# Fourier mixing by five products instead of six, border sums without a product of zeros, and one selection for layer 1's scale and shift

## The chip, the core and the metric

The kernel runs on one core of a Trainium2 chip. The metric is the time of one execution on the device in microseconds, the median of several runs. TensorE (PE) multiplies, VectorE (DVE) and ScalarE (ACT) work elementwise, GpSimd (POOL) does little here, SyncE (SP) issues most of the DMAs.

## The reference

Two layers of a diffusion trunk over 256 latent and 256 context tokens of width 2048. Each layer normalises, applies a scale and a shift that come from the conditioning vectors, projects, and mixes in three branches whose gated outputs go through one output projection:

```python
shift, scale, gate = jnp.split(silu_c @ w_mod[l] + b_mod[l], 3, axis=-1)
h = rmsnorm(x, g_pre[l]) * (1.0 + scale[:, None]) + shift[:, None]
proj = h @ w_in[l]                      # split into branches A, B, C and their gates
...
def fourier_mix(xc, w_f, b_f):          # branch C
    xg = xc.reshape(bsz, t, C_GROUPS, C_DIM).astype(jnp.float32)
    y = jnp.fft.fft2(xg, axes=(1, 3), norm='ortho').real.astype(xc.dtype)
    y = jnp.einsum('btgc,gcd->btgd', y, w_f) + b_f
...
y = rmsnorm(y @ w_out[l], g_post[l]);  x = x + gate[:, None] * y
```

The context stream gets the same in layer 0; in layer 1 it gives only keys and values.

## The kernel before

All activations lie transposed (features on partitions, 512 columns: latent, then context). Precision comes from splits: `split_into` writes the float32r high part of a float32 tensor with ScalarE (line 562 in the profile) and the low part by a subtraction on VectorE (line 563), and `mm3` multiplies high by high, high by low and low by high (lines 545, 546, 547). Weights arrive by DMA as `raw`, are split into `whi` (L513) and `wlo` (L515), and `tunit` or, in layer 1, `tunit1` (L692, L693) multiplies one unit of 128 output columns by all 16 tiles of the input.

TensorE works in program order. What isn't the main stream of units is put in between by `Later`: generators such as `fourier`, `attention`, `mod_end` and `boundary` yield a number, the time in microseconds of the main stream after which their next piece is issued. `YF` holds `fourier`'s numbers (3.4 us between the first and second stage in layer 0, 6.4 us in layer 1). On VectorE, ScalarE and SP the order after the first stage is made by priorities; every engine's queue is then in order.

Branch C's 2-D transform is two stages. `fourier_mats` multiplies the cosine and the sine matrix by the group's weight matrix, once per layer, and keeps high and low parts in `mg` and `mgl`. `fourier(g, ps)` runs once per group (4) and layer. It adds and subtracts mirrored positions (L1015), so that an even half `e` and an odd half `o` of 128 positions each stand for 256 positions, and splits them. Then for each stream (two in layer 0, one in layer 1) the first stage multiplies each half by cosine and sine together, 256 columns, by `mm3`: six products into the tile `ps_f`. Of the four blocks of 128 columns that come out, the second stage uses even by cosine, odd by sine, and of odd by cosine a single row, which takes the place of row 0 of the odd-by-sine block. A split of the two blocks and a split of the one row follow (ACT and DVE, each one operation of 128x256 and one of 1x128), and `ps_z` is six more products: three by `ct`, three by `nst`, the last of which needs the row's subtraction.

Layer 1's shift and scale and layer 0's gate are vector work: `mod_dve` multiplies 512 columns of `w_mod` with VectorE, at a low priority (`macc`, L292 and L294, with transposes and reductions into `red`, L300 and L301), as DMAs bring `mraw`. Four such blocks fill a `red` tile. `mod_end` then selects and turns them by eight small products (four `PE.matmul` of float32, two instructions each; tile `ps_modc`, L314), and `mod_cols` adds biases (L151, L155, L157). It is issued `MODEND` microseconds of main stream after the last block: 53 in layer 0, 45 in layer 1. It runs three times: for layer 0's gate, layer 1's scale (`gs`) and layer 1's shift (`sh`). The first layer-1 product needs both, in `make_h` (L623, L632).

Sums over features come from products with a column of ones: `col_sums` (L581, L583), called in `rms_of` for the context stream between the layers (twice), and the same by hand in `boundary` (L1359, L1362). Both open the accumulation with a product of ones by zeros over all columns, and add each column's product to it.

Of the kernel before, what the change touches and what calls it, by code (L numbers as in the profile page):

```python
# [7 lines left out]
F32 = mybir.dt.float32  # L8
F32R = mybir.dt.float32r
BF16 = mybir.dt.bfloat16  # L10
AF = mybir.ActivationFunctionType
ALU = mybir.AluOpType

P = 128
# [52 lines left out]
def trunk_kernel(ctx: ExitStack, tc: tile.TileContext, xT, xhalf, cT, wss, wsl, wmod, win, wout0, wout1, const, vec, rows,  # L67
                 wmat, bs, sink, out):
    nc = tc.nc
    V, A, G, PE, DMA = nc.vector, nc.scalar, nc.gpsimd, nc.tensor, nc.sync  # L70
# [6 lines left out]
    def sb(shape, dt, tag, bufs=1):  # L77
        cnt[0] += 1
        return pool.tile(shape, dt, tag=tag, bufs=bufs, name=f"{tag}_{cnt[0]}")
# [8 lines left out]
    def ms_ps(name="ms"):  # L88
        cnt[0] += 1
        return psum.tile([P, 512], F32, tag="ms", bufs=2, name=f"ps_{name}_{cnt[0]}")  # L90
# [6 lines left out]
    ones = sb([P, P], F32, "ones")  # L97
# [4 lines left out]
    zero8 = sb([P, 8], F32, "zero8")  # L102
    V.memset(zero8, 0.0)
    zero4 = zero8[:, 0:4]
# [22 lines left out]
    def cc(name):  # L127
        o, w = COFF[name]
        return cst[:, o - P:o - P + w]
# [151 lines left out]
    def mod_dve(l, cb, red):  # L281

        acc = sb([P, 2, 512], F32, "macc")
        for kg in range(4):
            for kk in range(4):
                if kk % 2 == 0:
                    w = sb([P, 2, 512], F32, "mraw", 2)
                    DMA.dma_start(w, wmod[(cb - 8) if l == 0 else 4 + cb, kg][:, kk:kk + 2])
                for s in range(2):
                    c = cs[:, kg * 4 + kk, s:s + 1]  # L290
                    if kg == 0 and kk == 0:
                        V.tensor_scalar(out=acc[:, s], in0=w[:, kk % 2], scalar1=c, scalar2=None, op0=ALU.mult)  # L292
                    else:
                        V.scalar_tensor_tensor(out=acc[:, s], in0=w[:, kk % 2], scalar=c, in1=acc[:, s],  # L294
                                               op0=ALU.mult, op1=ALU.add)
                if kk % 2 and (kg < 3 or kk < 3):
                    yield
        t = sb([P, 2, 512], F32, "mraw", 2)
        for s in range(2):
            V.transpose(t[:, s], acc[:, s])  # L300
            V.tensor_reduce(out=red[:, s], in_=t[:, s].rearrange("p (b j) -> p b j", j=32),  # L301
                            axis=mybir.AxisListType.X, op=ALU.add)
        yield

    def mod_four(l, cbs):
        red = sb([P, 4, 2, 16], F32, "red", 2)
        for i, cb in enumerate(cbs):
            yield from mod_dve(l, cb, red[:, i])
        later.add(mod_end(l, cbs, red), MODEND[l])

    def mod_end(l, cbs, red):
        ps = ms_ps("modc")
        for q in range(4):
            PE.matmul(ps[32 * q:32 * q + 32, 0:32], cc("selq"),  # L314
                      red.rearrange("p c s (j q) -> p c s j q", q=4)[:, :, :, :, q], start=True, stop=True,
                      tile_position=(0, 32 * q))
        for i, cb in enumerate(cbs):
            mod_cols(l, cb, ps[:, 8 * i:8 * i + 8].rearrange("p (s j) -> p j s", s=2))
        yield 0.0

# [30 lines left out]
        yield 0.0  # L351

    def mod_rest():
        yield from mod_four(0, range(8, 12))
        yield from mod_four(1, range(4, 8))
        yield from mod_four(1, range(0, 4))
        while "acc" not in state:
            yield
        yield from mod_gate1()
# [23 lines left out]
    MODEND = 53.0, 45.0  # L383
# [41 lines left out]
    later = Later()  # L425
# [118 lines left out]
    def mm3(ps, st, mv, start, stop):  # L544
        PE.matmul(ps, st[0], mv[0], start=start, stop=False)  # L545
        PE.matmul(ps, st[0], mv[1], start=False, stop=False)  # L546
        PE.matmul(ps, st[1], mv[0], start=False, stop=stop)  # L547

    def part(w, c):

        def of(t):
            if not isinstance(t, list):
                return t[:, c]
            n = t[0].shape[-1]
            return t[c.start // n][:, c.start % n:c.start % n + c.stop - c.start]

        return of(w[0]), of(w[1])
# [3 lines left out]
    def split_into(hi, lo, src):  # L561
        A.copy(hi, src)  # L562
        V.tensor_tensor(out=lo, in0=src, in1=hi.bitcast(F32), op=ALU.subtract)  # L563
        return hi, lo
# [10 lines left out]
        G.tensor_tensor(out=r[:, :n], in0=t[:, :n], in1=mhalf[:, :n], op=ALU.pow)  # L575
        return r

    def col_sums(ps, q, n, start=True, stop=True):

        if start:  # L580
            PE.matmul(ps[:, 0:n], ones, zero4[:, 0:n], start=True, stop=False)  # L581
        for j in range(n):
            PE.matmul(ps[:, j:j + 1], q[:, j * P:(j + 1) * P], ones[:, 0:1], start=False, stop=stop and j == n - 1)  # L583

    wz = sb([P, T], BF16, "join", 2)

# [137 lines left out]
    def layer(l):  # L724
        last = l == 1
        n = S if last else T
# [3 lines left out]
        if last:  # L730
            a = sb([P, 4, 256], F32, "macc")
            c = [sb([P, 2, S], F32, f"kt{j}") for j in range(2)]
# [50 lines left out]
        if l == 0:  # L783
            mod = {}
            for k in range(KT):
# [42 lines left out]
                m = mod.get(k + 1)  # L828
# [160 lines left out]
                yield (4.0 if h == 1 else 2.0) if l == 0 else (7.0 if h == 1 else 2.0)  # L989


        mg = sb([P, 4, 2, P], F32R, "mg"), sb([P, 4, 2, P], F32R, "mgl")

        wfp = sb([P, 1024], F32R, "vv")
        wfp = split_into(wfp[:, 0:512], wfp[:, 512:1024], wf.rearrange("p g d -> p (g d)"))
# [3 lines left out]
        def fourier_mats():  # L999
            for j in range(2):  # L1000
                ps = ms_ps("mg")
                mm3(ps, csp[j], wfp, True, True)
                split_into(mg[0][:, :, j], mg[1][:, :, j], ps.rearrange("p (g d) -> p g d", d=P))
            yield 0.0

        def fourier(g, ps):


            e = w2k([P, n // S, 2, P])
            p2 = ps[:, 0:n].rearrange("p (s t) -> p s t", t=S)  # L1010
            A.copy(e[:, :, :, 0:1], ps[:, 0:n].rearrange("p (s j t) -> p s j t", j=2, t=P)[:, :, :, 0:1])
            back = w2k([P, n // S, P])
            A.copy(back, p2[:, :, P:S])
            for j, op in enumerate((ALU.add, ALU.subtract)):
                V.tensor_tensor(out=e[:, :, j, 1:P], in0=p2[:, :, 1:P], in1=back[:, :, P - 1:0:-1], op=op)  # L1015
            x = split_into(w2k([P, n], F32R), w2k([P, n], F32R), e.rearrange("p s j t -> p (s j t)"))
            yield YF[l][0]
            z = mm_ps("z")
            mgg = [m[:, g].rearrange("p a b -> p (a b)") for m in mg]
            for s in range(n // S):  # L1020
                a = ms_ps("f1")
                for j in range(2):
                    t = 2 * s + j
                    mm3(a[:, j * 256:(j + 1) * 256], part(x, slice(t * P, (t + 1) * P)), mgg, True, True)
                a1 = w2k([P, 2, P], F32R), w2k([P, 2, P], F32R)
                split_into(*a1, a.rearrange("p (q d) -> p q d", d=P)[:, 0::3])
                split_into(a1[0][0:1, 1], a1[1][0:1, 1], a[0:1, 256:384])
                yield YF[l][1]
                zs = z[:, s * S:(s + 1) * S]
                for j, nm in enumerate(("ct", "nst")):  # L1030
                    mm3(zs, [m[:, j] for m in a1], split[nm], j == 0, j == 1)
            A.activation(ytmp(12 + g), z[:, 0:n], AF.Identity, bias=vc(l, "bf")[:, g:g + 1])
# [322 lines left out]
    def boundary(acc, cross):  # L1355


        ps = ms_ps("rs")
        PE.matmul(ps[:, 0:6], ones, zero8[:, 0:6], start=True, stop=False)  # L1359
        for i in range(6):  # L1360
            q = acc[:, i * P:(i + 1) * P] if i < 2 else cross[:, (i - 2) * P:(i - 1) * P]
            PE.matmul(ps[:, i:i + 1], q, ones[:, 0:1], start=False, stop=i == 5)  # L1362
        r = rstd_cols(ps[:, 0:2], 2, D)
        m, u = sb([P, 4], F32, "mx", 2), sb([P, 4], F32, "nm", 2)
        V.tensor_scalar(out=m[:, 0:2], in0=ps[:, 2:4], scalar1=2.0 / D, scalar2=None, op0=ALU.mult)
        V.tensor_scalar(out=m[:, 2:4], in0=ps[:, 4:6], scalar1=1.0 / D, scalar2=None, op0=ALU.mult)  # L1366
        for i, (x, op) in enumerate(((r[:, 0:2], ALU.mult), (m[:, 0:2], ALU.add), (r[:, 0:2], ALU.mult), (msx, ALU.add))):
            V.tensor_tensor(out=u[:, 0:2], in0=u[:, 0:2] if i else m[:, 2:4], in1=x, op=op)
        V.tensor_scalar(out=u[:, 0:2], in0=u[:, 0:2], scalar1=EPS, scalar2=None, op0=ALU.max)
        r1 = sb([P, 4], F32, "rs_b", 2)  # L1370
        G.tensor_tensor(out=r1[:, 0:2], in0=u[:, 0:2], in1=mhalf[:, 0:2], op=ALU.pow)
        yield YX[1]
        rb = bcast(r, 2)
        state["r0"] = sb([P, S], F32, "rbs", 2)
        A.copy(state["r0"], rb[:, 0:S])
        for k in range(NX):
            x1_of(k)
        yield YX[2]
        rb = bcast(r1, 2)
        rbs[0] = sb([P, S], F32, "rbs", 2)  # L1380
        A.copy(rbs[0], rb[:, 0:S])
# [54 lines left out]
    with tc.manual_schedule(engines={EN.PE}):  # L1436
# [11 lines left out]
        for k in range(KT):  # L1448
            q = w2k([P, T])
# [128 lines left out]
```

## Time and profile before

| | |
|---|---|
| median of 3 runs | 1126.23 us (1125.98 to 1126.52) |
| the profiled execution | 1126.57 us |
| its span in the trace | 1124.8 us |
| TensorE busy | 1116.0 us, 99% |
| VectorE busy | 919.9 us, 82% |
| ScalarE busy | 548.8 us, 49% |
| granted TensorE clock | 0.999 |

The profile is of one execution. A row of grouped instructions gives line, engine, operation, output and inputs, shapes and count; a row of the order of time gives start, duration, engine, line and operation, and in brackets how long the engine stood idle before it and for whom. `PEld` is TensorE's weight load. Matmul durations are pipelined: what one costs is the step to the next start, not its duration.

### The profile page before, as it was taken

The page shows a single profiled execution, that of the slowest core. Times are in us where ns is not written, and L with a number is a line of the kernel's source. Part 1 is how long each engine was busy: PE and PEld are TensorE (multiplying, and loading weights), DVE is VectorE, ACT ScalarE, POOL GpSimd, SP SyncE. Part 2 cuts the span into 40 slices and gives each one's busy share as a digit, 9 for nine tenths or more (in the row PEclk, how much of TensorE's full clock was granted, in tenths as well). Part 3 has the DMA queues.
Part 4 walks back from the last instruction along what each step waited for, and adds up shares of the span by engine and source line. Part 5 has one row for each costly group of instructions (what it writes and reads, how often), then busy time and mean ns, then how long its engine had stood idle before and what let it go on. Part 6 is the DMA issues. An engine that isn't in the chain of part 4 may idle for free.

```text
span 1124.8 us, 16564 instructions
## 1 busy us (share of the span) xinstructions
PE 1116.0 (99%) x6069; PEld 919.4 (82%) x6072; DVE 919.9 (82%) x1573; ACT 548.8 (49%) x1044; POOL 34.9 (3%) x44
## 2 busy tenths in 40 slices
PE   8999999999999999999999999999999999999998
PEld 3666788888888888888888888988888888898886
DVE  2667699899988897988998989396989689878883
ACT  5454723322335667632533334266665369867551
POOL 0000000000000000000000000030500000000000
PEclk9999999999999999999999999999999999999999
DMA  9999755576655343465566665285946686456872
GB/s 360 402 401 399 258 165 173 168 241 206 212 189 182 112 152 121 128 202 186 169 194 206 218 207 186 95 197 193 236 154 204 211 294 198 159 180 200 302 254 75
DMA packets 76002, 235.84 MB, mean 210 GB/s; under 512 B 8704, under 2 KB 13200, under 8 KB 75920
## 3 DMA queue, kind: packets, MB, share of 16 engines
q1 hardware_dynamic: 71136, 229.79, 60.7%
q0 software_dynamic: 4064, 3.69, 2.2%
q10 hardware_dynamic: 720, 1.31, 0.3%
q8 instruction: 47, 0.77, 0.3%
q14 instruction: 35, 0.29, 0.1%
HBM read 232.65 MB, written 2.10 MB: 209 GB/s over the span
## 4 chain that ended last, share of the span: by engine, by line
PE 88%; DVE 5%; DMA 3%; ACT 2%; issue 1%; ACTq 0%; POOLq 0%; DVEq 0%; SPq 0%
PE ps_t L545 14%; PE ps_t L547 14%; PE ps_t L546 14%; PE ps_t L692 9%; PE ps_t L693 5%; PE ps_av L771 4%; PE ps_v L1174 3%; PE ps_y L545 3%; PE ps_y L547 3%; PE ps_y L546 3%; PE ps_mod L182 2%; DVE macc L294 2%; DVE wlo L515 1%; PE ps_v L1175 1%; PE ps_tp L1116 1%; DMA mraw<-in_wmod_dram 1%
## 5 line engine op out<-in xcount | busy, mean ns | idle before, releaser
L513 ACT CAST whi<-raw 128x1024 fp32r<-128x1024 f32 (+1 forms) x209 | 215.9, 1037 | 314.7 <-PE ps_t L546 214.0
L545 PE MATMUL ps_t<-hh,whi 128*128 128x512 f32 (+1 forms) x752 | 290.7, 387 | 0.0
L515 DVE TENSOR_TENSOR wlo<-raw,whi 128x1024 fp32r<-128x1024 f32 (+1 forms) x209 | 250.4, 1202 | 48.3 <-ACT whi L513 40.5
L546 PE MATMUL ps_t<-hl,whi 128*128 128x512 f32 (+1 forms) x752 | 289.6, 385 | 0.0
L547 PE MATMUL ps_t<-hh,wlo 128*128 128x512 f32 (+1 forms) x752 | 289.4, 385 | 0.0
L294 DVE SCALAR_TENSOR_TENSOR macc<-mraw,cs,macc 128x512 f32<-128x512 f32 x360 | 250.5, 744 | 14.6 <-DMA mraw<-in_wmod_dram 14.1
L692 PE MATMUL ps_t<-hh,whi 128*128 128x512 f32 x512 | 184.6, 399 | 0.0
L547 PEld LDWEIGHTS ps_t<-hh,wlo 128*128 128x128 f32 x752 | 141.3, 188 | 28.7
L545 PEld LDWEIGHTS ps_t<-hh,whi 128*128 128x128 f32 x752 | 141.3, 188 | 26.7
L546 PEld LDWEIGHTS ps_t<-hl,whi 128*128 128x128 f32 x752 | 141.3, 188 | 26.3
L693 PE MATMUL ps_t<-hh,wlo 128*128 128x256 f32 x512 | 143.4, 280 | 0.0
L692 PEld LDWEIGHTS ps_t<-hh,whi 128*128 128x128 f32 x512 | 96.1, 188 | 21.2
L693 PEld LDWEIGHTS ps_t<-hh,wlo 128*128 128x128 f32 x512 | 96.7, 189 | 0.4
L545 PE MATMUL ps_y<-whi,hh 128*128 128x512 f32 x104 | 41.3, 397 | 0.0
L547 PE MATMUL ps_y<-whi,hh 128*128 128x512 f32 x104 | 40.6, 391 | 0.0
L546 PE MATMUL ps_y<-wlo,hh 128*128 128x512 f32 x104 | 40.5, 389 | 0.0
L562 ACT CAST w2k<-ps_tp 128x512 fp32r<-128x512 f32 x40 | 23.4, 584 | 21.2 <-PE ps_scc L546 13.7
L575 POOL TENSOR_TENSOR rs_b<-rs_a,mhalf 128x2 f32<-128x2 f32 (+1 forms) x6 | 6.7, 1115 | 759.5 <-DVE mx L1366 584.6
L563 DVE TENSOR_TENSOR w2k<-ps_tp,w2k 128x512 fp32r<-128x512 f32 x40 | 27.4, 684 | 3.5 <-ACT w2k L562 2.3
L1096 ACT ACTIVATE w2k<-w2k,den 128x512 f32<-128x512 f32 (+1 forms) x48 | 28.1, 647 | 0.7 <-DVE den L1091 0.6
L188 DVE STREAM_TRANSPOSE w2k<-ps_mod 128x256 f32<-128x256 f32 (+1 forms) x15 | 7.0, 468 | 26.1 <-PE ps_mod L182 24.5
L771 PE MATMUL ps_av<-whi,hh 128*128 128x512 f32 x64 | 24.6, 397 | 0.0
(483 smaller groups left out, 1819.3 us busy)
## 6 DMA issues: line engine op xcount, KB each, us to landing
raw<-in_win_dram SPq DMA_DIRECT2D x158, 512.0 KB, 4.1
mraw<-in_wmod_dram SPq DMA_DIRECT2D x128, 512.0 KB, 4.4
raw<-in_wout_dram SPq DMA_DIRECT2D x60, 512.0 KB, 4.5
mraw<-in_wsl_dram SPq DMA_DIRECT2D x12, 512.0 KB, 7.3
mg<-in_wsl_dram SPq DMA_DIRECT2D x7, 512.0 KB, 9.0
mgl<-in_wsl_dram SPq DMA_DIRECT2D x7, 512.0 KB, 9.0
yo<-in_xhalf_dram POOLq DMA_DIRECT2D x28, 128.0 KB, 7.2
yo<-in_xT_dram SPq DMA_DIRECT2D x12, 256.0 KB, 4.9
```

The lines of the kernel that those rows point to most:

```text
L294: V.scalar_tensor_tensor(out=acc[:, s], in0=w[:, kk % 2], scalar=c, in1=acc[:, s], op0=ALU.mult, op1=ALU.add)
L513: A.copy(ph, rc)
L515: self.last = V.tensor_tensor(out=pl, in0=rc, in1=ph.bitcast(F32), op=ALU.subtract)
L545: PE.matmul(ps, st[0], mv[0], start=start, stop=False)
L546: PE.matmul(ps, st[0], mv[1], start=False, stop=False)
L547: PE.matmul(ps, st[1], mv[0], start=False, stop=stop)
L563: V.tensor_tensor(out=lo, in0=src, in1=hi.bitcast(F32), op=ALU.subtract)
L692: PE.matmul(ps, w[0], h, start=k == 0, stop=False)
L693: PE.matmul(ps[:, 0:S], w[1], h[:, 0:S], start=False, stop=k == KT - 1)
L771: PE.matmul(ps, st[a], mv[b], start=start and (a, b) == (0, 0), stop=stop and (a, b) == (1, 0))
L1096: A.activation(prob[i][:, b * w:(b + 1) * w], prob[i][:, b * w:(b + 1) * w], AF.Copy, scale=den[:, c:c + 1])
L1174: PE.matmul(vps[t], hi, wk, start=k == 0, stop=False)
```

## The change

1. `fourier`'s first stage takes five products. The matrices are stored per pair of groups in the order sine high, cosine high, cosine low, sine low. The even half's high part is multiplied by cosine high and cosine low side by side (256 columns, blocks 0 and 1), its low part by cosine high alone (128 columns, added to block 0); even by sine is not formed. The odd half has its three products of 256 columns, into blocks 2 and 3. Block 1 is added to the low part of block 0's split by one VectorE operation. `fourier_mats` writes each product in two copies and two subtractions, one for each pair of groups.
2. `col_sums` and `boundary` lose the product of zeros; each column's product opens and closes its own accumulation.
3. Layer 1's scale and shift blocks are selected in one `mod_end`, at the place of the later one; layer 0's gate as before.

```diff
-    def mod_four(l, cbs):
-        red = sb([P, 4, 2, 16], F32, "red", 2)
-        for i, cb in enumerate(cbs):
-            yield from mod_dve(l, cb, red[:, i])
-        later.add(mod_end(l, cbs, red), MODEND[l])
-
-    def mod_end(l, cbs, red):
+    def mod_fours(l, *fours):
+        reds = []
+        for cbs in fours:
+            reds.append(sb([P, 4, 2, 16], F32, "red", 2))
+            for i, cb in enumerate(cbs):
+                yield from mod_dve(l, cb, reds[-1][:, i])
+        later.add(mod_end(l, fours, reds), MODEND[l])
+
+    def mod_end(l, fours, reds):
         ps = ms_ps("modc")
-        for q in range(4):
-            PE.matmul(ps[32 * q:32 * q + 32, 0:32], cc("selq"),
-                      red.rearrange("p c s (j q) -> p c s j q", q=4)[:, :, :, :, q], start=True, stop=True,
-                      tile_position=(0, 32 * q))
-        for i, cb in enumerate(cbs):
+        for i, red in enumerate(reds):
+            for q in range(4):
+                PE.matmul(ps[32 * q:32 * q + 32, 32 * i:32 * i + 32], cc("selq"),
+                          red.rearrange("p c s (j q) -> p c s j q", q=4)[:, :, :, :, q], start=True, stop=True,
+                          tile_position=(0, 32 * q))
+        for i, cb in enumerate(cb for cbs in fours for cb in cbs):
             mod_cols(l, cb, ps[:, 8 * i:8 * i + 8].rearrange("p (s j) -> p j s", s=2))
...
     def mod_rest():
-        yield from mod_four(0, range(8, 12))
-        yield from mod_four(1, range(4, 8))
-        yield from mod_four(1, range(0, 4))
+        yield from mod_fours(0, range(8, 12))
+        yield from mod_fours(1, range(4, 8), range(0, 4))
...
-    def col_sums(ps, q, n, start=True, stop=True):
-
-        if start:
-            PE.matmul(ps[:, 0:n], ones, zero4[:, 0:n], start=True, stop=False)
+    def col_sums(ps, q, n):
+
         for j in range(n):
-            PE.matmul(ps[:, j:j + 1], q[:, j * P:(j + 1) * P], ones[:, 0:1], start=False, stop=stop and j == n - 1)
+            PE.matmul(ps[:, j:j + 1], q[:, j * P:(j + 1) * P], ones[:, 0:1], start=True, stop=True)
...
-        mg = sb([P, 4, 2, P], F32R, "mg"), sb([P, 4, 2, P], F32R, "mgl")
+        mg = [sb([P, 2, 4, P], F32R, tag) for tag in ("mg", "mgl")]
...
                 mm3(ps, csp[j], wfp, True, True)
-                split_into(mg[0][:, :, j], mg[1][:, :, j], ps.rearrange("p (g d) -> p g d", d=P))
+                for i in range(2):
+                    split_into(mg[i][:, :, 1 - j], mg[i][:, :, 2 + j],
+                               ps[:, i * 256:(i + 1) * 256].rearrange("p (g d) -> p g d", d=P))
...
-            mgg = [m[:, g].rearrange("p a b -> p (a b)") for m in mg]
+            m = mg[g // 2][:, g % 2]
             for s in range(n // S):
-                a = ms_ps("f1")
-                for j in range(2):
-                    t = 2 * s + j
-                    mm3(a[:, j * 256:(j + 1) * 256], part(x, slice(t * P, (t + 1) * P)), mgg, True, True)
+                a = ms_ps("f1").rearrange("p (q d) -> p q d", d=P)
+                xe, xo = (part(x, slice(t * P, (t + 1) * P)) for t in (2 * s, 2 * s + 1))
+                PE.matmul(a[:, 0:2], xe[0], m[:, 1:3], start=True, stop=False)
+                PE.matmul(a[:, 0], xe[1], m[:, 1], start=False, stop=True)
+                mm3(a[:, 2:4], xo, (m[:, 0:2], m[:, 3:1:-1]), True, True)
                 a1 = w2k([P, 2, P], F32R), w2k([P, 2, P], F32R)
-                split_into(*a1, a.rearrange("p (q d) -> p q d", d=P)[:, 0::3])
-                split_into(a1[0][0:1, 1], a1[1][0:1, 1], a[0:1, 256:384])
+                split_into(*a1, a[:, 0::2])
+                V.tensor_tensor(out=a1[1][:, 0], in0=a1[1][:, 0].bitcast(F32), in1=a[:, 1], op=ALU.add)
+                split_into(a1[0][0:1, 1], a1[1][0:1, 1], a[0:1, 3])
...
         ps = ms_ps("rs")
-        PE.matmul(ps[:, 0:6], ones, zero8[:, 0:6], start=True, stop=False)
         for i in range(6):
             q = acc[:, i * P:(i + 1) * P] if i < 2 else cross[:, (i - 2) * P:(i - 1) * P]
-            PE.matmul(ps[:, i:i + 1], q, ones[:, 0:1], start=False, stop=i == 5)
+            PE.matmul(ps[:, i:i + 1], q, ones[:, 0:1], start=True, stop=True)
```

## The prediction

> **What bounds the kernel now.** I read the page's busy shares, the waits of TensorE, then the order of time around each edited place.
>
> ```profile
> span 1124.8 us, 16564 instructions
> PE 1116.0 (99%) x6069; PEld 919.4 (82%) x6072; DVE 919.9 (82%) x1573; ACT 548.8 (49%) x1044; POOL 34.9 (3%) x44
> PEclk9999999999999999999999999999999999999999
> PE ps_idle L590 <- DVE red L112: 2.0, 1, 2.0
> PE ps_x L1315 <- ACT w2k L1307: 0.5, 1, 0.5
> PE ps_z L547 <- DVE w2k L563: 0.2, 1, 0.2
> ```
>
> PE is busy in 99% of the span at a full granted clock throughout. The last three rows are three of PE's seven waits (engine, line, awaited instruction: total us, times, longest). The first and the four not shown, of 0.5 us and less, belong to the opening stage, L1315 to the last output tile. Between the two only one product waited, 0.2 us: the last of Fourier's second stage. So what a change takes out of PE's stream comes off the end, unless a product then waits for VectorE. All three parts are priced on PE; the extra work on VectorE is priced by whether a product waits for it.
>
> **Part 1, Fourier's products.** `fourier` multiplies per group and stream (8 times in layer 0, 4 in layer 1) six products of 256 moving columns now.
>
> ```profile
> 167.10 0.28 PE L545 MATMUL ps_f<-mg,w2k 128*128 128x256 f32 x1
> 167.69 0.28 PE L547 MATMUL ps_f<-mg,w2k 128*128 128x256 f32 x1
> 167.81 0.40 PE L545 MATMUL ps_t<-hh,whi 128*128 128x512 f32 x1
> 797.72 0.28 PE L545 MATMUL ps_f<-mg,w2k 128*128 128x256 f32 x1
> 798.29 0.28 PE L547 MATMUL ps_f<-mg,w2k 128*128 128x256 f32 x1
> ```
>
> From 167.10 to the next tile's first product at 167.81 are six steps: 0.118 us each (the 0.28 is a pipelined duration, not a price). In layer 1 five steps take 0.57: 0.114 each. Afterwards there are four products of 256 columns and one of 128. No float32r product of 128 columns is in this trace. The nearest rows are float32 products with all 128 weights: those with one moving column (L583), and those with 128 (L982).
>
> ```profile
> 823.68 0.28 PE L693 MATMUL ps_t<-hh,wlo 128*128 128x256 f32 x1
> 823.68 0.31 PEld L581 LDWEIGHTS ps_rs<-zero,ones 128*128 128x128 f32 x2
> 823.91 0.53 PEld L583 LDWEIGHTS ps_rs<-ones,acc 128*128 128x128 f32 x4
> 824.36 0.19 PEld L692 LDWEIGHTS ps_t<-hh,whi 128*128 128x128 f32 x1
> 147.07 1.05 PE L982 MATMUL ps_mix<-ws,w2k 128*128 128x128 f32 x8
> ```
>
> Four weight loads for single columns start at 823.91 and the next tile's at 824.36: 0.112 each, with almost nothing to stream. So 0.112 is the floor that loading 128 weights sets. L982's eight instructions are four float32 products, two instructions each: (1.05 - 0.28) / 7 = 0.11 an instruction, taking 0.28 for the last one's duration, so 0.22 a product. A float32r product of 128 columns therefore costs between 0.112 (one instruction, weight load decides) and 0.22 (as float32). I take 0.112: the float32r products in the first fence are one instruction each, and even at 256 columns they are within 0.006 of that floor. Saved: 8 x (2 x 0.118 - 0.112) + 4 x (2 x 0.114 - 0.112) = 0.99 + 0.46 = 1.45 us. At the other end: 8 x 0.014 + 4 x 0.006 = 0.14 us.
>
> The Trainium skill, "TensorE: Matmul & The Clock Gate", section "LDWEIGHTS (loading the stationary operand)", prices a load by its columns over 1.2, 107 ns for 128, which the 0.112 here bears out; but its section "Back-to-back issue gap" gives about 81 ns for a load and product of 128 columns, by which the estimate of this part would be 8 x 0.155 + 4 x 0.147 = 1.83 us. The float32 rows above do not show such a step.
>
> **Part 2, border sums.** Three calls lose the product of zeros: L581 twice (the context stream's sums) and L1359 once (the boundary). Its two loads run from 823.68 to 823.91, 0.23 us; 3 x 0.23 = 0.69 us. It waits for nothing before or behind it, so all of it is PE's.
>
> **Part 3, the selection in one place.** Layer 1's two sets of eight small products become sixteen in one place.
>
> ```profile
> 556.83 0.39 PE L547 MATMUL ps_t<-hh,wlo 128*128 128x512 f32 x1
> 557.15 0.31 PE L314 MATMUL ps_modc<-red,cst 128*32 128x32 f32 x8
> 557.39 0.50 PE L545 MATMUL ps_t<-hh,whi 128*128 128x512 f32 x1
> 557.73 0.40 PE L546 MATMUL ps_t<-hl,whi 128*128 128x512 f32 x1
> 557.96 0.39 PE L547 MATMUL ps_t<-hh,wlo 128*128 128x512 f32 x1
> 697.69 0.31 PE L314 MATMUL ps_modc<-red,cst 128*32 128x32 f32 x8
> L314 PE MATMUL ps_modc<-red,cst x24: 224/229/235, 377.3 to 697.8; 128*32 128x32 f32 x24
> L151 DVE TENSOR_TENSOR sh<-ps_modc,vecs x4: 154/154/158, 698.8 to 699.0; 128x8 f32<-128x8 f32 x4
> L623 DVE SCALAR_TENSOR_TENSOR w2k<-yo,gs,rbs x16: 477/481/485, 731.7 to 757.6; 128x256 f32<-128x256 f32 x16
> ```
>
> From 556.83 to 557.73 are 0.90 us, where two ordinary steps (0.23, as from 557.73 to 557.96) would take 0.46: an excursion costs 0.44. The eight themselves step by (0.31 - 0.23) / 7 = 0.011, so putting eight more behind the set at 697.69 adds 0.1, and the earlier excursion goes: 0.34 us saved. The scale now arrives with the shift, some 1 us later than 699 with its operations in the vector queue, and is first read at 731.7: over 30 us of cover. If that were gone, every layer-1 product would wait for it.
>
> **What is added on VectorE.** Per group and stream one addition of 128x128 (PSUM operand), twelve in all; and `fourier_mats` makes four narrower copies and four subtractions where it made two and two. Rows for the addition: an L1065 operation of that shape takes 0.29 us, and the one-partition subtraction of 128 occupies 0.20 (170.61 to 170.81).
>
> ```profile
> L1065 DVE TENSOR_TENSOR ps_sc<-ps_sc,m0r 128x128 f32<-128x128 f32 x32 | 8.7, 290 | 1.8 <-PE ps_sc L547 1.8
> 170.61 0.27 DVE L563 TENSOR_TENSOR w2k<-ps_f,w2k 1x128 fp32r<-1x128 f32 x1
> 170.81 4.70 DVE L294 SCALAR_TENSOR_TENSOR macc<-mraw,cs,macc 128x512 f32<-128x512 f32 x7
> 191.33 0.27 DVE L563 TENSOR_TENSOR w2k<-ps_f,w2k 1x128 fp32r<-1x128 f32 x1
> 191.69 0.19 PEld L547 LDWEIGHTS ps_z<-nstrh,w2k 128*128 128x128 f32 x1
> 202.22 0.40 DVE L563 TENSOR_TENSOR w2k<-ps_f,w2k 128x256 fp32r<-128x256 f32 x1
> 204.34 1.42 DVE L294 SCALAR_TENSOR_TENSOR macc<-mraw,cs,macc 128x512 f32<-128x512 f32 x2 [1.72 <-DMA mraw<-in_wmod_dram]
> 205.68 0.27 DVE L563 TENSOR_TENSOR w2k<-ps_f,w2k 1x128 fp32r<-1x128 f32 x1
> 206.00 0.39 PE L547 MATMUL ps_z<-nstrh,w2k 128*128 128x256 f32 x1 [0.25 <-DVE w2k L563]
> 219.61 0.27 DVE L563 TENSOR_TENSOR w2k<-ps_f,w2k 1x128 fp32r<-1x128 f32 x1
> 219.94 0.38 PE L547 MATMUL ps_z<-nstrh,w2k 128*128 128x256 f32 x1
> 805.18 0.27 DVE L563 TENSOR_TENSOR w2k<-ps_f,w2k 1x128 fp32r<-1x128 f32 x1
> 806.76 0.28 PE L547 MATMUL ps_z<-nstrh,w2k 128*128 128x256 f32 x1
> 160.00:180.00 20.00, 20.00 (x105) 17.10 (x105) 18.39 (x31) 6.90 (x14) 0.00 (x0) 1.00 0.52 181
> ```
>
> The addition waits for nothing new on PE (its column block is done before the odd half's products) and stands ahead of the row's subtraction in program order. Behind it in the vector queue are that subtraction, the weight splits (L515) and layer 0's modulation sums (L294); the last product of the second stage waits for the subtraction. In layer 1 the subtraction ends at 805.45, over a microsecond ahead of its product at 806.76. In layer 0 VectorE is over 90% busy (the last row's third figure, 18.39 of 20 us) and three of the eight places have almost no room: at 191.69 (0.09 after 191.60), at 206.00 (the wait itself) and at 219.94. There the subtraction stands behind two L294, which waited 1.72 us for their DMA in the case shown.
>
> Nothing to lose is one end: the additions run in such gaps and only push back the modulation sums. The other end: the queue keeps its order, and where it isn't waiting for a DMA each addition delays all behind it by 0.2; in the order of time I count five such of the eight, so by 220 the subtraction, and with it PE, is 1.0 us later than before, whatever PE saved until then. Then layer 0's 0.99 is lost and 1.0 more with it. I take 0.4 us of new waits, one addition's 0.2 at each of the two places with no room at all, nearest to the 0.25 that the one such wait costs now; the additions are urgent work, and a sum of the modulation is what the order puts behind it.
>
> ```profile
> L547 PE MATMUL ps_mg<-vv,w2k x4: 392/393/398, 137.8 to 773.9; 128*128 128x512 f32 x4
> ```
>
> The narrower copies have from 773.9, the last product for the matrices, to 797.72, their first use in layer 1, and as long in layer 0. If that cover were gone they would cost two more operations of 0.20 on VectorE, 0.4 us a layer.
>
> **The sum.** 1.45 + 0.69 + 0.34 - 0.4 = 2.1 us. The profiled execution took 1126.57 us around its span of 1124.8, 0.34 above the median of 1126.23. 1126.57 - 2.1 = 1124.5 in its terms, 1124.1 as a median.
>
> **The rivals.**
> - *No wait is added:* 2.5 us, and the 0.25 at 206 may go too: 1123.5 to 1123.75. For it: VectorE idles beside L294's waits for DMA. Against: three subtractions have under 0.1 us of room.
> - *VectorE sets layer 0's end:* +1.0 there, less 0.46 in layer 1, 0.69 and 0.34: 0.5 us gained, 1125.7. For it: the queue is in order and 92% busy. Against: it idles 1.72 us ahead of 204.34, which absorbs additions before it.
> - *A product of 128 columns costs 0.22,* as float32: 0.14 + 0.69 + 0.34, less at most 0.4: 0.8 to 1.2 gained, 1125.0 to 1125.4. For it: the kernel has no float32r product below 256 columns to deny it. The Trainium skill, "FP8 and Floating Point Precision", section "TensorE Precision Notes", counts four passes for true float32, which would fit L982's double price; it doesn't say that float32r of few columns is taken so.
> - *Slower:* with the additions in it, the vector queue of layer 0 gets another order, and at each of the three tight places two more L294 stand ahead of the row's subtraction: 2 x 0.67 (the seven from 170.81 take 4.70) and a wait for their DMA of 1.72, 3.06 us a place. Three places are 9.2 us, less 2.5: 1132.9; two give 1129.8; one costs 0.6 more than is gained. It decides from two places on. For it: this already happened at 204.34. Against: once in eight.
>
> **How the numbers follow.** A measurement of this kernel can tell about 0.2% (2.25 us: below 1123.98, above 1128.48) from no change. My forecast with waits between none and 0.9 us, the first rival in it, has 0.56 (1123.5 to 1124.6); it straddles the bound, 0.40 below it and 0.16 above. VectorE sets layer 0's end 0.12; the dear narrow product 0.20; slower 0.12. Faster 0.40, same 0.48, slower 0.12. The low end, 1123.2, is the first rival's 1123.5 less the runs' scatter of 0.3 (1125.98 to 1126.52 about the median). The high end, 1126.4, is both middle rivals together (a loss of 1.0 in layer 0 against 0.02 in layer 1, 0.69 and 0.34: 1126.2) and 0.2 of scatter. The slower case and a small rest are left out.
>
> **What would show it.** Right: five ps_f products per group and stream, the 128-column one stepping by 0.11; 60 of them, not 72; no zero loads in the border sums, 0.45 us from first load to the next tile's; one set of 16 L314-like products near 697 and eight near 377; PE's waits for ps_z under 0.7 us. Wrong: a step of 0.22 or two instructions at the narrow product; ps_z waits of over 1 us in layer 0; PE idle in places that the change doesn't touch, which would mean that the queues' order changed as a whole.

## The result, and the profile after

The changed kernel takes 1128.59 us (20 runs, 1126.84 to 1131.38), the kernel before, measured alongside, 1126.56 (20 runs, 1125.85 to 1128.72). The ratio is 1.0019, 95% interval 1.0013 to 1.0026: slower by 2.0 us, where 2.1 less were forecast. The profiled execution took 1127.61 us, with a span of 1125.8.

The page of the changed kernel, its span and its busy shares:

```profile
span 1125.8 us, 16570 instructions
PE 1114.5 (99%) x6054; PEld 917.3 (81%) x6054; DVE 922.9 (82%) x1589; ACT 549.9 (49%) x1048; POOL 34.1 (3%) x44
```

TensorE has 1.5 us less to do than before (1116.0), and the span is 1.0 longer. So 2.5 us of new idle time on TensorE have to be found. Its waits, as total, times and longest:

```profile
PE ps_idle L590 <- DVE red L112: 2.0, 1, 2.0
PE ps_mask L961 <- issue: 1.8, 1, 1.8
PE ps_z L549 <- DVE w2k L565: 0.8, 2, 0.4
PE ps_mix L982 <- issue: 0.3, 1, 0.3
```

The first row was there before. The third is the wait that was forecast, somewhat larger: 0.8, where under 0.7 was named as the sign of being right. The second and the fourth are new, in front of products that the change does not touch: the transpose of attention's mask (L961, layer 0) and branch A's first mixing product of layer 1 (L982). "issue" means that the profile shows nothing for which TensorE waited.

Three windows of the changed kernel: the mask, layer 0's second stage, layer 1. The first figure after the length is TensorE's busy time; before it was 10.00, 59.75 and 60.00.

```profile
140.00:150.00 10.00, 8.22 (x40) 6.59 (x39) 9.04 (x17) 4.75 (x10) 1.02 (x1) 1.00 0.36 120
165.00:225.00 60.00, 59.20 (x302) 50.25 (x300) 54.26 (x96) 20.71 (x40) 0.00 (x0) 1.00 0.52 167
770.00:830.00 60.00, 59.66 (x364) 52.72 (x363) 49.74 (x105) 39.96 (x87) 17.40 (x19) 1.00 0.76 205
```

1.78, 0.80 and 0.34 us idle. What happens at the mask is read from the order of time of the changed kernel:

```profile
138.86 0.40 PE L549 MATMUL ps_mg<-vv,w2k 128*128 128x512 f32 x1
139.24 0.41 ACT L564 CAST mg<-ps_mg 128x256 fp32r<-128x256 f32 x1
...
140.12 0.42 ACT L564 CAST mg<-ps_mg 128x256 fp32r<-128x256 f32 x1
...
141.41 0.42 DVE L565 TENSOR_TENSOR mg<-ps_mg,mg 128x256 fp32r<-128x256 f32 x1
...
141.81 0.42 DVE L565 TENSOR_TENSOR mg<-ps_mg,mg 128x256 fp32r<-128x256 f32 x1
141.86 0.77 ACT L564 CAST mgl<-ps_mg 128x256 fp32r<-128x256 f32 x2 [0.37 <-DVE mg L565]
...
143.03 1.68 DVE L977 TENSOR_SCALAR w2k<-w2k,rs_b 128x512 f32<-128x512 f32 x4 [0.81 <-POOL rs_b L577]
144.62 0.75 DVE L565 TENSOR_TENSOR mgl<-ps_mg,mgl 128x256 fp32r<-128x256 f32 x2
145.11 0.14 PEld L961 LDWEIGHTS ps_mask<-identr,w2k 128*128 128x128 f32 x1 [2.17 <-issue]
145.14 0.30 PE L961 MATMUL ps_mask<-identr,w2k 128*128 128x128 f32 x1 [1.78 <-issue]
```

And the same place before:

```profile
139.09 0.68 DVE L563 TENSOR_TENSOR mgl<-ps_mg,mg 128x512 fp32r<-128x512 f32 x1
...
140.05 0.69 DVE L563 TENSOR_TENSOR mgl<-ps_mg,mg 128x512 fp32r<-128x512 f32 x1
...
142.07 1.67 DVE L977 TENSOR_SCALAR w2k<-w2k,rs_b 128x512 f32<-128x512 f32 x4 [0.91 <-POOL rs_b L575]
...
142.85 0.27 PE L961 MATMUL ps_mask<-identr,w2k 128*128 128x128 f32 x1
```

`ps_mg`, `ps_mask` and `ps_mix` are small PSUM tiles (tiles into which products are written) of one tag, allocated by `ms_ps` with two buffers. The two products of `fourier_mats` take both, so the next small tile, whatever it is for, has to wait until the first one's readers are done. Before, these were one copy and one subtraction, over by 139.77. Afterwards they are two of each, and the second copy (`mgl`, 141.86) starts only when the first half's subtraction of that tile has ended (141.41 + 0.42 = 141.83), though it reads another half. The two subtractions of `mgl` then come behind the four scalings of branch A's tile (L977), which themselves stand for 0.81 us waiting for POOL. The pair starts at 144.62, and one such subtraction takes 0.42 (as at 141.41); so the first is over at 145.04, and the mask's weight load starts 0.07 behind it, at 145.11.

That ScalarE's copy and VectorE's subtraction of one tile take turns is what the Trainium skill, "PSUM — Partial Sum Buffer", section "PSUM bank collisions raise a hardware error", asks for: accesses of two engines to the same 32 partitions of one bank have to be kept apart by semaphores, reads against reads and disjoint columns included. The wait of 0.37 us above agrees with it.

Layer 1 has the same shape, with one addition (L699, from 779.39) between the halves in place of the scalings: the subtractions of `mgl` start at 779.72, the first is over at 780.14, and the first mixing product's weight load starts at 780.21, again 0.07 behind. The profile itself does not name the buffer; the reading rests on the allocation, on this coincidence in both layers, and on the kernels halves, mask_later and split_early below.

```profile
779.18 0.70 ACT L564 CAST mgl<-ps_mg 128x256 fp32r<-128x256 f32 x2 [0.16 <-DVE mg L565]
779.72 0.75 DVE L565 TENSOR_TENSOR mgl<-ps_mg,mgl 128x256 fp32r<-128x256 f32 x2
780.24 0.68 PE L982 MATMUL ps_mix<-ws,w2k 128*128 128x128 f32 x4 [0.34 <-issue]
```

The same product in both traces, start against start, gives the account of the 1.0 us by which the span grew. A positive step is time lost:

| place | step, us |
|---|---|
| opening, a product that waits for a DMA at 28 | +0.32 |
| mask's transpose | +2.0 |
| eight first stages of layer 0 | 8 x -0.12 |
| last product of a second stage, at 191.81, 206.00 and 219.94 | +0.14, +0.12, +0.54 |
| one selection goes (557), the other grows (697) | -0.45, +0.12 |
| three border sums (724, 783, 823) | 3 x -0.22 |
| layer 1's first mixing product | +0.58 |
| four first stages of layer 1 | 4 x -0.11 |
| all else (a step of -0.14 at 765 the largest) | -0.2 |

The gains stand where they were forecast, 2.4 us together. The mask and the mixing product take 2.6, the second stages 0.8.

### The profile page after: what moved, and what is told of

It reads as the page before. It is cut to its first block, busy times and chain, and to the rows that moved or that the text cites. A ratio compares the mean times of both kernels' runs of the same rounds, so it can differ in the third digit from the quotient of the medians.

```text
span 1125.8 us, 16570 instructions
## 1 busy us (share of the span) xinstructions
PE 1114.5 (99%) x6054; PEld 917.3 (81%) x6054; DVE 922.9 (82%) x1589; ACT 549.9 (49%) x1048; POOL 34.1 (3%) x44
## 4 chain that ended last, share of the span: by engine, by line
PE 91%; DVE 3%; DMA 2%; ACT 2%; issue 1%; ACTq 0%; POOLq 0%; DVEq 0%; SPq 0%
PE ps_t L547 15%; PE ps_t L549 15%; PE ps_t L548 15%; PE ps_t L692 9%; PE ps_t L693 5%; PE ps_av L771 4%; PE ps_v L1178 3%; PE ps_y L547 3%; PE ps_y L549 3%; PE ps_y L548 3%; PE ps_mod L182 2%; PE ps_v L1179 1%; PE ps_tp L1120 1%; PE ps_au L547 1%; DVE wlo L517 1%; DMA yo<-in_xT_dram 1%
```

## The experiments

**The theory** after the result: cutting the matrices' evacuation in halves holds two buffers longer, and the next small tile waits. **The rivals:** the additions and their wait in the second stage make the loss; or the two kernels' vector queues differ in general, so that any edit of `fourier` would give some gap. The first four kernels share a run of the kernel before of 1126.84 us (30 runs), the next four one of 1126.75 (31 runs), the last three one of 1126.45 (15 runs).

**halves**: the kernel before with nothing but the cut evacuation.

```diff
-                split_into(mg[0][:, :, j], mg[1][:, :, j], ps.rearrange("p (g d) -> p g d", d=P))
+                for i in range(2):
+                    split_into(mg[0][:, 2 * i:2 * i + 2, j], mg[1][:, 2 * i:2 * i + 2, j],
+                               ps[:, i * 256:(i + 1) * 256].rearrange("p (g d) -> p g d", d=P))
```

> The kernel before, with one thing of the change: each product of the matrices is written by two copies and two subtractions of two groups each instead of one and one of four; products, border sums and selection stay as before. Bank theory (the narrower splits hold the two PSUM banks longer, because the second copy waits for the first subtraction and the last subtractions fall behind the scaling of branch A's tile in VectorE's queue, and the mask's transpose waits for a bank): a gap of PE of about 1.8 us at the mask's transpose and 0.3 to 0.7 us at layer 1's first mix product, so 2 to 3 us slower than before, 1128.5 to 1129.5. Addition theory (the twelve additions on VectorE cause the loss): within 0.5 us of before, 1126.1 to 1127.1, and no gap at the mask.

Measured: 1129.02 us (10 runs), ratio 1.0022 (1.0013 to 1.0032). Its waits of TensorE hold both new rows:

```profile
PE ps_mask L961 <- issue: 1.5, 1, 1.5
...
PE ps_mix L982 <- issue: 0.3, 1, 0.3
```

The edit leaves six products, no addition, both selections and the zeros: none of the change's gains, and none of its cost but this one. It is enough for 2.2 us. Its order of time has the scalings at 142.69, the second subtractions behind them at 144.29, and the mask's product at 144.80. No second stage waits in it, where the kernel before had one wait of 0.2.

**no_fourier**: the change with `fourier`, `fourier_mats` and the matrices' layout as before; only the border sums and the selection remain.

```diff
-        mg = [sb([P, 2, 4, P], F32R, tag) for tag in ("mg", "mgl")]
+        mg = sb([P, 4, 2, P], F32R, "mg"), sb([P, 4, 2, P], F32R, "mgl")
...
```

> The change without its first part: Fourier's products, matrices and splits as before; border sums without the product of zeros and the selection in one place. Both the bank theory and the addition theory: faster by what the two small parts take out of PE, 0.69 + 0.34 = 1.0 us, 1125.5. If one of the small parts moves the order of a queue to its harm: slower than 1126.5.

Measured: 1125.82 us (11 runs), ratio 0.9992 (0.9983 to 1.0001), not told apart from no change by its interval. The median gains 1.02, which is what the forecast had for these two parts (0.69 + 0.34). No wait at L961 or L982. But its second stages wait more than before's 0.2, and it has no additions:

```profile
PE ps_z L549 <- DVE w2k L565: 0.7, 2, 0.5
```

At the longer of the two, VectorE waited 2.69 us for a DMA and took two modulation sums (190.64) ahead of the row's subtraction (191.98). So a wait there does not need an addition.

**fourier_alone**: the other part, the kernel before with the new `fourier` and `fourier_mats`.

```diff
-        mg = sb([P, 4, 2, P], F32R, "mg"), sb([P, 4, 2, P], F32R, "mgl")
+        mg = [sb([P, 2, 4, P], F32R, tag) for tag in ("mg", "mgl")]
...
```

> The kernel before with the change's first part alone (Fourier's five products with the new matrices and the addition). Bank and addition theory: 1.0 us over the changed kernel, 3 us over before, 1129.6; by the ledger of the two traces -1.4 for products, +2.1 at the mask, +0.7 at the mix, +0.5 in the second stage, +1.9 in all, 1128.5. If the selection or the border sums cost something: less than the changed kernel.

Measured: 1129.51 us (9 runs), ratio 1.0021 (1.0010 to 1.0032). TensorE waits 1.6 us at the mask and 0.3 at the mixing product. The loss comes with Fourier's part.

**mask_later**: the change, with the mask's transpose issued 3 us of main stream later.

```diff
-            later.add(turn_mask(), 7.0)
+            later.add(turn_mask(), 10.0)
```

> The changed kernel with one number changed: the transpose of the mask is put 10 instead of 7 us of main stream behind the start of layer 0's branches. Bank theory: PE no longer waits at the mask, 2.1 us less than the changed kernel, about 1126.5 where that is 1128.6. Addition theory: no difference, 1128.6. If PE's gap came from fetching instructions (the profile names no releaser), it moves along or stays at its time: 1128.6.

Measured: 1127.15 us (11 runs), ratio 1.0004 (0.9995 to 1.0013). The wait at the mask is gone, so it did not come from fetching instructions. By the medians 1.4 us came back, where the theory had 2.1. In the profiled execution, 0.9 above its median, nothing did: its span is 1126.3. Its waits of TensorE tell why:

```profile
PE ps_z L549 <- DVE w2k L565: 1.5, 4, 0.5
...
PE ps_mix L982 <- issue: 0.3, 1, 0.3
```

Four second stages now wait, 1.5 us together, where the changed kernel had two and 0.8. These idle times understate it, since the products behind a wait step more slowly too. Counted from each second stage's first product to the product behind its last, the twelve take 8.5 us where none waits (halves), 9.1 in the kernel before, 10.0 in the changed one and 12.0 here: the 2.0 us of the mask are lost again. With the gap at the mask TensorE reaches the second stages 2 us late, and VectorE has that much more time; in halves, with the gap, even the wait of the kernel before is gone. So the two losses cover each other in part, and the account above shows only what of the second is left over. How much varies from one execution to the next, as changed_look_1 and changed_look_2 show.

How the second stage loses is seen in the order of time of the changed kernel, at the place that was at 206.00 before:

```profile
205.47 0.75 DVE L294 SCALAR_TENSOR_TENSOR macc<-mraw,cs,macc 128x512 f32<-128x512 f32 x1 [1.14 <-DMA mraw<-in_wmod_dram]
206.14 0.28 DVE L1030 TENSOR_TENSOR w2k<-w2k,ps_f 128x128 fp32r<-128x128 f32 x1
206.34 1.22 DVE L517 TENSOR_TENSOR wlo<-raw,whi 128x1024 fp32r<-128x1024 f32 x1
206.51 0.26 ACT L564 CAST w2k<-ps_f 1x128 fp32r<-1x128 f32 x1 [1.87 <-DVE w2k L1030]
207.47 0.27 DVE L565 TENSOR_TENSOR w2k<-ps_f,w2k 1x128 fp32r<-1x128 f32 x1
...
207.80 0.39 PE L549 MATMUL ps_z<-nstrh,w2k 128*128 128x256 f32 x1 [0.36 <-DVE w2k L565]
```

The row's copy on ScalarE waits for the addition, though it reads another block of the tile: the same taking of turns. The row's subtraction can only come after that copy, and in the meantime VectorE takes a weight split of 1.22 us. The addition's 0.20 thus becomes 0.20 and a weight split: 206.14 to 207.47. The addition itself stands behind a modulation sum that waited 1.14 us for its DMA, so not all of the lateness is the addition's. At 220.38 the same order is found again.

**split_early**: the change, with both copies of a product issued first, then both subtractions, all at an urgent priority. The layout and the count of operations stay.

```diff
-                for i in range(2):
-                    split_into(mg[i][:, :, 1 - j], mg[i][:, :, 2 + j],
-                               ps[:, i * 256:(i + 1) * 256].rearrange("p (g d) -> p g d", d=P))
+                with low(-100):
+                    src = [ps[:, i * 256:(i + 1) * 256].rearrange("p (g d) -> p g d", d=P) for i in range(2)]
+                    for i in range(2):
+                        A.copy(mg[i][:, :, 1 - j], src[i])
+                    for i in range(2):
+                        V.tensor_tensor(out=mg[i][:, :, 2 + j], in0=src[i],
+                                        in1=mg[i][:, :, 1 - j].bitcast(F32), op=ALU.subtract)
```

> The changed kernel; fourier_mats alone is different: for each product both copies come first, then both subtractions, and the four get a higher priority, so that they stand ahead of the scaling of branch A's tile in VectorE's queue. Nothing else moves. Bank theory: no gap of PE at the mask nor at layer 1's first mix product, 2.8 us gone; but with PE 2 us earlier in layer 0 the second stage waits for the additions and the rows behind them, as it did with the mask put later (four waits of 0.4 us), so 1.0 to 1.5 us is given back: 1126.8 where the changed kernel is 1128.6. If the second stage's waits were only the mask's doing: 1125.6.

Measured: 1125.19 us (11 runs), ratio 0.9985 (0.9976 to 0.9994): faster than before by 1.6 us. The order of time at the mask:

```profile
141.56 0.42 DVE L1008 TENSOR_TENSOR mg<-ps_mg,mg 128x256 fp32r<-128x256 f32 x1
141.90 0.41 DVE L1008 TENSOR_TENSOR mgl<-ps_mg,mgl 128x256 fp32r<-128x256 f32 x1
...
142.81 0.27 PE L961 MATMUL ps_mask<-identr,w2k 128*128 128x128 f32 x1
...
144.28 0.49 DVE L977 TENSOR_SCALAR w2k<-w2k,rs_b 128x512 f32<-128x512 f32 x1 [0.91 <-POOL rs_b L577]
```

The first tile's readers end at 142.31, ahead of the scalings, and the mask's product finds its buffer free. The first subtraction is as late as in the changed kernel (141.56 against 141.41, where before had 139.09), so that lateness alone does not make the gap. With the same four operations for each product both gaps are gone, so it is not the narrower copies' own time that cost; and the new `fourier` is all in it, so the rival of a general difference falls too. Whether the order or the priority did it was not separated. The expectation had 1126.8, or 1125.6 if no wait came in place of the gap; the median is below both. One second-stage wait of 0.3 us is listed, but the twelve second stages take 10.9 us, 0.9 more than in the changed kernel: a part of the gain is given back there.

**split_early_row_first**: split_early, with the row's split ahead of the addition.

```diff
+                split_into(a1[0][0:1, 1], a1[1][0:1, 1], a[0:1, 3])
                 V.tensor_tensor(out=a1[1][:, 0], in0=a1[1][:, 0].bitcast(F32), in1=a[:, 1], op=ALU.add)
-                split_into(a1[0][0:1, 1], a1[1][0:1, 1], a[0:1, 3])
```

> As split_early, and the split of the single row is put ahead of the addition of block 1, so that the row's copy no longer waits for the addition. If the row's chain (split, addition, row's copy, row's subtraction) is what the second stage waits for, its waits fall by the addition's 0.2 to 0.3 us at each of the four places: 0.8 to 1.2 us less than split_early, 1125.8. If the additions' time in VectorE's queue is what counts, wherever they stand: the same as split_early, 1126.8.

Measured: 1124.70 us (11 runs), ratio 0.9984 (0.9975 to 0.9993). Layer 0's waits are gone: its eight second stages take 5.7 us, as where none waits, against 7.8 in split_early, and every addition is still made. With one execution of each, this points to the row's place behind the addition, rather than the additions' time, as what cost there. The medians differ by only 0.5 us, where 0.8 to 1.2 was expected, and their intervals overlap. One wait appears in layer 1, where now the addition is the last:

```profile
PE ps_z L549 <- DVE w2k L1034: 0.6, 1, 0.6
```

**no_addition**: split_early without the addition; block 1 is never added, so that part of the even half's product is left out.

```diff
-                V.tensor_tensor(out=a1[1][:, 0], in0=a1[1][:, 0].bitcast(F32), in1=a[:, 1], op=ALU.add)
```

> As split_early, with the addition left out: block 1 (even half high by cosine low) is computed and never added, so that part of the result is missing. The price of the additions alone. If they cause the second stage's waits: 1.0 to 1.5 us less than split_early, 1125.4, and as few waits for VectorE as before (0.2 us). If something else in the new order of the queue causes them: as split_early.

Measured: 1125.42 us (12 runs), ratio 0.9990 (0.9981 to 0.9998), no better than split_early; the span is 0.9 shorter (1123.0), and a wait of 0.5 us for the row's subtraction stays, behind two modulation sums (203.59) for which VectorE waited 1.78 us. The second stages take 9.5 us against 10.9, in one execution each; the changed kernel alone ranges from 9.7 to 10.8 over three. The medians do not show a price of the additions. Inconclusive for them.

**split_early_stage_later**: split_early, with layer 0's second stage issued 1.2 us of main stream later.

```diff
-    YF = [5.6, 3.4], [6.6, 6.4]
+    YF = [5.6, 4.6], [6.6, 6.4]
```

> As split_early, and layer 0's second stage of Fourier comes 4.6 instead of 3.4 us of main stream after the first (one number of YF). If the second stage's waits are only a matter of room, they vanish: 1.0 to 1.5 us less than split_early, 1125.4, and 2.4 to 2.7 less than before where nothing else gives way would be 1124.2. If VectorE's queue in layer 0 is itself the bound, the lateness goes on to the next places (the bank of ps_f, the weight splits): as split_early, 1126.8.

Measured: 1124.00 us (8 runs), ratio 0.9980 (0.9970 to 0.9990), the lowest median of all, 2.75 us under the kernel before and 1.2 under split_early, though the two intervals overlap. The same three windows:

```profile
140.00:150.00 10.00, 10.00 (x50) 8.37 (x49) 9.09 (x18) 4.49 (x10) 1.12 (x1) 1.00 0.49 161
165.00:225.00 60.00, 60.00 (x308) 51.37 (x307) 55.66 (x98) 19.92 (x40) 0.00 (x0) 1.00 0.47 167
770.00:830.00 60.00, 60.00 (x367) 53.21 (x367) 50.77 (x109) 38.20 (x84) 17.50 (x19) 1.00 0.70 202
```

TensorE stands idle in none of them, and the span is 1121.5, 3.3 less than before. The three parts make 2.4 of it, as in the account above. The second stages make 0.65 (8.5 us against 9.1): the kernel before's own wait goes as well, and its price is more than the 0.25 of idle time that the forecast read. The remaining 0.2 is spread over the span. The 0.65 belongs to the later second stage; whether it would help the kernel before by itself was not tried.

**changed_look_1** and **changed_look_2**: the changed kernel, unedited, for two more profiled executions.

> The changed kernel once more, one profiled execution: the first one's time (1127.61) is one of the lowest of 20, and its ledger explains 1.0 us against before where the medians differ by 2.0. If the gap at the mask varies with when VectorE comes to the splits (it waited 1.2 us for a DMA just ahead of them), the gap differs from 1.8 us by as much as the execution's time differs from 1127.6. If the rest lies elsewhere: the gap is 1.8 us again and the time is lost in the opening stage or spread over the span.

> A second execution of the changed kernel, as changed_look_1: a gap at the mask that moves with the execution's time, or one of 1.8 us again and the time lost in the opening stage.

Measured: 1127.65 and 1126.59 us, spans 1125.9 and 1124.8. The wait at the mask is 1.4 us in both: it neither follows the time nor stays at 1.8, so neither expectation is borne out. The second stages' waits differ:

```profile
PE ps_z L549 <- DVE w2k L565: 1.2, 3, 0.5
```

is the row of the first; in the second it is one wait of 0.5. The second stages take 10.8 and 9.7 us, 1.1 apart, as the times are. The gap is in each profiled execution; what differs between these two is the second stages.

**early_row_first_later**: split_early_row_first and the later second stage together.

```diff
-    YF = [5.6, 3.4], [6.6, 6.4]
+    YF = [5.6, 4.6], [6.6, 6.4]
```

> split_early with both remedies, the row's split ahead of the addition and layer 0's second stage at 4.6 us. split_early_stage_later left no wait of the second stage at all, so the order of row and addition has nothing to give in layer 0; in layer 1 row first alone had one new wait of 0.6 us. The same as split_early_stage_later or up to 0.6 us slower: 1124.0 to 1124.6 where before is 1126.75.

Measured: 1125.01 us (11 runs), ratio 0.9984 (0.9975 to 0.9993): outside the 1124.0 to 1124.6 that were expected, though the interval overlaps that of split_early_stage_later. The one wait listed, 0.3 us, is for the addition (L1034), and it is in layer 0 now, at 180.54. With the row first it is the addition that comes last; the later second stage alone leaves no such wait.

## Why the prediction was wrong

**The step that failed** is "The narrower copies have from 773.9 ... to 797.72, their first use in layer 1, and as long in layer 0. If that cover were gone they would cost ... 0.4 us a layer." On that ground the sum put the narrower copies at nothing. It took the matrices' reader for the one that ends the cover. But an evacuation, the operations that empty a PSUM tile, also frees its buffer, and the next one to want that comes much earlier: the mask's transpose was at 142.85 in layer 0, 4 us behind the last product for the matrices, and `ps_mix` at 778.35 in layer 1. The price was wrong too. It counted two operations of 0.20 on VectorE, where the loss is made by what stands in the queue between the two halves: 2.0 us in layer 0, 0.58 in layer 1. The halves kernel shows it alone: 2.2 us for this edit and nothing else.

**The addition.** The forecast called the addition's place "ahead of the row's subtraction" and let it delay the row's subtraction by its own 0.20 and took 0.4 us in all. The chain is longer: split, addition, the row's copy on ScalarE, the row's subtraction, and a weight split slips in. The second stages cost 0.8 us more than before in the profiled execution, 1.7 and 0.5 in the two others, and 2.8 in mask_later, without the gap. At 0.4 the term was below each of these, and it is not independent of the first mistake. What of it is the additions' own stays open: no_fourier has no additions and its second stages cost 0.6 more than before.

**The rivals.** The slower one had the right sign for a wrong reason: two modulation sums ahead of the row's subtraction, 3.06 us a place. What came ahead at two of the three named places was one weight split, for 0.4 us each, and that alone would not have made the kernel slower. *VectorE sets layer 0's end* had 1.0 us for layer 0; mask_later's second stages show a loss of that kind, 2.8 us, but in split_early_stage_later the same additions cost nothing once the stage comes 1.2 us later, so VectorE is not the bound of the layer. No rival named a buffer. Of the signs of being wrong, "PE idle in places that the change doesn't touch" came true, though not because the queues' order changed as a whole: one tag's two buffers were held longer. *No wait is added* gave 1123.5 to 1123.75, which is near what split_early_stage_later reaches (1124.00, measured beside a kernel before that is 0.5 above the median of the three runs shown).

**What was right.** The product of 128 columns is one instruction at the weight load's floor, and the dear product falls. In the changed kernel:

```profile
169.43 0.28 PE L1025 MATMUL ps_f<-mg,w2k 128*128 128x256 f32 x1
169.55 0.22 PE L1026 MATMUL ps_f<-mg,w2k 128*128 128x128 f32 x1
169.61 0.33 PE L547 MATMUL ps_f<-mg,w2k 128*128 128x256 f32 x1
169.78 0.28 PE L548 MATMUL ps_f<-mg,w2k 128*128 128x256 f32 x1
169.89 0.28 PE L549 MATMUL ps_f<-mg,w2k 128*128 128x256 f32 x1
170.01 0.40 PE L547 MATMUL ps_t<-hh,whi 128*128 128x512 f32 x1
```

Five steps take 0.58 us; 4 x 0.118 + 0.112 = 0.584 was forecast. Twelve sets saved 8 x 0.12 + 4 x 0.11 = 1.40 against 1.45. The border sums saved 0.67 against 0.69; the profile has only L583's four products left:

```profile
824.83 0.53 PEld L583 LDWEIGHTS ps_rs<-ones,acc 128*128 128x128 f32 x4
...
825.28 0.19 PEld L692 LDWEIGHTS ps_t<-hh,whi 128*128 128x128 f32 x1
```

0.45 us, as forecast. The selection saved 0.33 against 0.34. Its sixteen products took 0.43 us where eight had taken 0.31.

**What stays open.** The medians differ by 2.0 us and the profiled executions by 1.0. The changed kernel's three profiled executions (1127.61, 1127.65, 1126.59) all lie about 1 us or more below its median of 1128.59, while the kernel before was profiled at its median. Where the timed runs lose the other microsecond no trace shows. The distance does not go with the gap alone: fourier_alone has it (1127.39 against 1129.51), halves in part (1128.37 against 1129.02), but so has split_early_stage_later without the gap (1123.29 against 1124.00), and split_early does not (1125.65 against 1125.19). A lower granted clock goes with the longest times only. Eight of the changed kernel's twenty runs show 0.997 or 0.998, with a median of 1130.0; the other twelve, at 0.999 or 1.000, still have 1128.5. Such a clock is found in 14 of the 41 runs of the kernels with the gap at the mask (the changed kernel with its two further executions, halves and fourier_alone), in one of 75 of the other edits, and in none of the 76 runs of the kernel before whose clock is on record. None of the profiled executions has it, so why it goes with the gap is not shown.

## What to carry to other kernels

An operation that empties a PSUM tile has two deadlines, the first reader of what it writes and the next taker of the buffer; price a cut or a delay of it against the earlier one. When TensorE's idle time is put down to "issue" at a product that nobody edited, list the tiles of its tag in program order, count back as many as the tag has buffers, and find that tile's last reader. And a wait that is removed shows the waits behind it, so test it together with the place that is late next.

## What was not expected of the hardware

The 128-column product does not step evenly: the next product starts 0.06 us after it, and the one behind that 0.17 later, where 256 columns step 0.11 to 0.12. Over the two the mean is 0.115, close to the 0.112 by which the weight loads of L583 step in the forecast. The Trainium skill, "TensorE: Matmul & The Clock Gate", section "Back-to-back issue gap", gives about 81 ns for a load and product of 128 columns. For float32r this trace does not agree: 0.58 us for the set, where four steps of 0.118 and one of 0.081 would make an estimate of 0.55.
